# A hybrid decoder layer on one core: an early rope rotation on GpSimd, its casts behind the first query, and both heads' transposes ahead of the state products

## The chip, the cores and the metric

The kernel runs on one NeuronCore of a Trainium2 chip. The metric is device time in microseconds of one execution, from runs on the chip. The engines are TensorE (PE, matmuls and transposes; its weight loads are listed as PEld), VectorE (DVE), ScalarE (ACT), GpSimd (POOL) and SyncE (SP, which only issues DMAs here). Each engine works through its own queue in order; engines wait for one another through semaphores.

## The reference

One layer on 512 tokens of width 1024. Two branches read the same normalised input: HGRN2, a gated linear recurrence with 8 heads of 128, and multi-head latent attention (MLA) with 8 heads. Both are gated and merged; a projection, the residual and a last norm follow.

```python
h = rms_norm(x, norm_g[l]); proj = h @ w_in[l]
hq, hf, hi, hz, cq, ckv, kr, mz, glog = jnp.split(proj, pts, axis=-1)
y_a = hgrn2_branch(hq, hf, hi, hz, lower_bounds[l], hg_norm_g[l])
y_b = mla_branch(cq, ckv, kr, mz, ...)
merged = gates[:, :, 0] * (y_a @ w_proj_a[l]) + gates[:, :, 1] * (y_b @ w_proj_b[l])
x = x + merged @ w_out[l]
...
# HGRN2, in chunks of 32 tokens, per head
f = lb + (1 - lb) * sigmoid(hf); q = silu(hq); k = 1 - f; log_f = log(f)
b = cumsum(log_f)                                  # within a chunk
q_in, k_in, k_out = q * exp(b), k * exp(-b), k * exp(b_last - b)
o_intra = tril(q_in k_in^T) v
state = state * decay + k_out^T v;  o_inter = q_in state
...
# MLA: queries with a rope part of 64 columns per head
q_nope = q[..., :128];  q_pe = apply_rope(q[..., 128:], cos, sin)
s = (q_nope k_nope^T + q_pe k_pe^T) * scale; p = softmax(s); out = p v
```

`apply_rope` turns pairs of columns: x1 cos - x2 sin, x2 cos + x1 sin.

## The kernel before

Channels lie on the 128 partitions and the 512 tokens on the free axis. Large products are made from float32 split in two parts (`hi`, a cast on ScalarE at L118, and `lo`, a subtraction on VectorE at L119); `mm3` issues three matmuls (L91 to L93) for each pair of blocks. Weights come through `load_w`: a DMA into one of 3 raw buffers, then the two parts into one of 4 buffers each.

After the start, the HGRN2 heads are worked two at a time by `hg_pair` (pairs 0 to 3). A pair projects the forget gates (`pf`), runs `hg_forget` for each head, projects the values (in pairs 0 and 2) or the gate `z` (in 1 and 3), projects the queries and runs `hg_query` for each head, then `hg_states`, `hg_scores`, `hg_out` and `hg_gate`.

- `hg_forget`: tanh on ScalarE (L455), `f` on VectorE, `k` and `fr` on GpSimd (L458, L457), a scan and a reciprocal on VectorE (L460, L461), nine tiny products of chunk decays on GpSimd (`gh`, `ft`, L466 to L474), then `ki`, `ko` and `k128` on VectorE and `k64` on GpSimd (L478). `tf`, `f` and `k` have one buffer each.
- `hg_query`: tanh (L486), then `q`, `qi`, `q128` on VectorE and `q64` on GpSimd (L490).
- `hg_states`, one head: three transposes of `k128` on PE (L499), one ScalarE copy of the result to `kt` (L500, one buffer), three products with the values on PE (L504), and the running sums `st` on VectorE (L505, L508).
- `hg_scores`: three groups of small matmuls (L518, L524, L529) and four masked copies on VectorE (L533). `hg_out` (L542, L544) reads their result and `st`.

PSUM is used in banks of 128x512 float32: 3 for `mm_tile` (projections) and 5 for `ax_tile` (the rest), given out in turn.

The MLA queries' rope part is made for two heads at once. `mla_turn` projects it (`qr`) and makes a copy with swapped halves through DMAs from ScalarE's queue (`qs`). `mla_rotate` makes the rotation on GpSimd: two products with the table (L637, L638), their sum (L639), and two DMAs from GpSimd's queue that swap the partition halves into `qx`, which takes the buffer of `qs` (L642). `mla_rope` makes the parts that matmuls read: on ScalarE a cast of `qx` to `qh` (L650) and of the halves of `qr` to `qp` (L653), on VectorE two subtractions (L654). `mla_nope` makes the other query part and the keys of one head: 15 matmuls, and casts `qn`, `kn`.

For the first pair of MLA heads this is done inside the last HGRN2 pair: `mla_turn(0)` before it, the rotation as `after_forget` (behind both heads' `hg_forget`), and `mla_rope` and `mla_nope(0)` as `before_gate` (behind `hg_states`). `step` issues, from GpSimd's queue, DMAs that add blocks of later weights to one another in DRAM (L767).

The order on each queue is set when the program is built, by a list scheduler with its own cost estimates; only where the code says `manual_schedule` or `issue_after` is it bound by hand. `last_pool`, `last_act` and `last_dve` hold instructions behind which an `issue_after` places others.

Of the kernel before, what the change touches and what calls it, by code (L numbers as in the profile page):

```python
# [14 lines left out]
ALU = mybir.AluOpType  # L15
# [3 lines left out]
P = 128  # L19
D = 1024  # L20
S = 512
NT = S // P
KD = D // P
H = 8
# [14 lines left out]
def hybrid_layer(ctx: ExitStack, tc: tile.TileContext, a):  # L39
    nc = tc.nc  # L40
# [16 lines left out]
    def ax_tile():  # L57
        return ax.tile([P, 512], F32, tag="ax", name="ax_ps")
# [68 lines left out]
    def proj_ch(mat, c0, rhs, hook=None):  # L127

        ps = [mm_tile() for _ in range(2)]
        for kh, w in enumerate(load_cols(mat, c0)):  # L130
            for m in range(2):
                if hook and kh and m:
                    hook()
                for k in range(4):
                    kk = 4 * kh + k
                    mm3(ps[m][:], w, rhs, (slice(None), k, slice(m * P, m * P + P)),
                        (slice(None), kk), kk == 0, kk == KD - 1)
        return ps
# [17 lines left out]
    last_pool, last_dve, last_act = [None], [None], [None]  # L156
# [247 lines left out]
    kt = cw.tile([P, NT, NR], F32, "kt")  # L404
# [31 lines left out]
    for i in range(2):  # L436
        gh = hw.tile([P, NT, 12], F32, f"gh{i}")
# [5 lines left out]
    W = lambda tag, bufs=2, shape=(P, S): hw.tile(list(shape), F32, tag, bufs)  # L443
# [4 lines left out]
    def bc(gh, o, n):  # L448
        return gh[:, :, o : o + n].rearrange("p g (n o) -> p g n o", o=1).broadcast_to([P, NT, n, C])

    def hg_forget(h, pf):

        gh = gh_[h % 2]
        tf, f, k = W("tf", 1), W("f", 1), W("k", 1)
        nc.scalar.activation(tf[:], pf[:], AF.Tanh, scale=0.5)  # L455
        nc.vector.tensor_scalar(f[:], tf[:], c1[:, h : h + 1], c2[:, h : h + 1], op0=ALU.mult, op1=ALU.add)
        nc.gpsimd.tensor_scalar(fr[:, ::C], f[:, ::C], TINY, None, op0=ALU.max)  # L457
        nc.gpsimd.tensor_scalar(k[:], tf[:], c1n[:, h : h + 1], c1[:, h : h + 1], op0=ALU.mult, op1=ALU.add)  # L458
        pr, rp = W("pr"), W("tf", 1)
        nc.vector.tensor_tensor_scan(pr[:], f[:], fr[:], 0.0, op0=ALU.mult, op1=ALU.max)  # L460
        nc.vector.reciprocal(rp[:], pr[:])  # L461
        last = pr[:, C - 1 :: C]
        F = last.rearrange("p (g c) -> p g c", c=4)

        g = nc.gpsimd
        cp = lambda o, i: g.tensor_copy(gh[:, :, o], F[:, :, i])  # L466
        ml = lambda o, x, y: g.tensor_tensor(gh[:, :, o], x, y, op=ALU.mult)
        cp(2, 3), cp(5, 0), cp(8, 1), cp(11, 2)
        ml(1, F[:, :, 2], F[:, :, 3])
        ml(0, F[:, :, 1], gh[:, :, 1])  # L470
        ml(6, F[:, :, 0], F[:, :, 1])
        ml(7, gh[:, :, 6], F[:, :, 2])
        ft = W("ft", 2, (P, NT))
        g.tensor_tensor(ft[:], gh[:, :, 6], gh[:, :, 1], op=ALU.mult)  # L474
        ki, ko, k128, k64 = W("ki"), W("ko"), W("k128"), W("k64", 2, (P, S // 2))
        nc.vector.tensor_tensor(ki[:], k[:], rp[:], op=ALU.mult)
        nc.vector.tensor_tensor(c3(ko), c3(ki), last.rearrange("p (n o) -> p n o", o=1).broadcast_to([P, S // C, C]), op=ALU.mult)
        last_pool[0] = g.tensor_tensor(c2_(k64), c4(ko)[:, :, 0:2], bc(gh, 8, 2), op=ALU.mult)  # L478
        nc.vector.tensor_tensor(c4(k128), c4(ko), bc(gh, 0, 4), op=ALU.mult)
        return pr, ft, ki, ko, k64, k128  # L480

    def hg_query(h, pq, pr):

        gh = gh_[h % 2]
        q = W("f", 1)
        last_act[0] = nc.scalar.activation(q[:], pq[:], AF.Tanh, scale=0.5)  # L486
        nc.vector.scalar_tensor_tensor(q[:], q[:], 1.0, pq[:], op0=ALU.add, op1=ALU.mult)
        qi, q128, q64 = W("qi"), W("q128"), W("q64", 2, (P, S // 2))
        nc.vector.tensor_tensor(qi[:], q[:], pr[:], op=ALU.mult)
        last_pool[0] = nc.gpsimd.tensor_tensor(c2_(q64), c4(qi)[:, :, 2:4], bc(gh, 10, 2), op=ALU.mult)  # L490
        last_dve[0] = nc.vector.tensor_tensor(c4(q128), c4(qi), bc(gh, 4, 4), op=ALU.mult)
        return qi, q64, q128

    def hg_states(h, k128, ft, v_sb):

        kps, kt_ = ax_tile(), W("kt", 1)
        n3 = 3 * P
        for i in range(NT - 1):
            nc.tensor.transpose(kps[:, i * P : i * P + P], k128[:, i * P : i * P + P], ident[:])  # L499
        nc.scalar.copy(kt_[:, :n3], kps[:, :n3])  # L500
        sps, st_ = ax_tile(), W("st", 2, (P, n3))
        for i in range(NT - 1):
            sl = slice(i * P, i * P + P)
            nc.tensor.matmul(sps[:, sl], kt_[:, sl], v_sb[i][:, (h % 4) * P : (h % 4) * P + P], start=True, stop=True)  # L504
        nc.vector.tensor_copy(st_[:, 0:P], sps[:, 0:P])  # L505
        for i in range(1, NT - 1):
            sl, sp = slice(i * P, i * P + P), slice(i * P - P, i * P)
            nc.vector.scalar_tensor_tensor(st_[:, sl], st_[:, sp], ft[:, i : i + 1], sps[:, sl], op0=ALU.mult, op1=ALU.add)  # L508
        return st_
# [55 lines left out]

    v_sb = [None] * NT

    def hg_pair(pair, after_forget=None, before_gate=None, last=None):
        cc, hs = pair * 256, (2 * pair, 2 * pair + 1)
        pf = proj_ch(w_in, COL_F + cc, hT)  # L570
        kk = [hg_forget(h, pf[i]) for i, h in enumerate(hs)]
        if after_forget:
            after_forget()
        if pair:
            step()
        else:
            early_sums(kh[0])
        def gate():
            pz = proj_ch(w_in, COL_ZA + cc, hT)
            zz = [z_tile() for _ in hs]  # L580
            for i in range(2):
                silu2(zz[i][:], pz[i][:])
            return zz

        if pair % 2 == 0:
            for t in range(NT):
                v_sb[t] = hw.tile([P, 512], F32, f"v{t}")
            proj_tok(w_in, COL_I + cc, hT, lambda t, ps: nc.scalar.copy(v_sb[t][:], ps[:]))
        else:
            zz = gate()  # L590
        pq = proj_ch(w_in, COL_Q + cc, hT)
        qq = [hg_query(h, pq[i], kk[i][0]) for i, h in enumerate(hs)]
        step()
        sts = [hg_states(h, kk[i][5], kk[i][1], v_sb) for i, h in enumerate(hs)]
        if before_gate:
            before_gate()
        if pair % 2 == 0:
            zz = gate()
        def scores():
            return hg_scores([(h, kk[i][2:5] + qq[i][0:2]) for i, h in enumerate(hs)])  # L600

        def outs(aa):
            on = [hg_out(h, aa[i], sts[i], qq[i][2], v_sb) for i, h in enumerate(hs)]
            step()
            return on

        def gated(on):
            for i, h in enumerate(hs):
                hg_gate(h, on[i], zz[i])

        if last:
            return last(scores, outs, gated)
        gated(outs(scores()))
# [29 lines left out]
        last_pool[0] = turn  # L643
        return qr, qx

    def mla_rope(qr, qx):

        qp, qh = [ma_pool.tile([P, S], F32R, f"qp{i}") for i in range(2)], ma_pool.tile([P, S], F32R, "qh")
        with tc.issue_after(last_act[0].ins), tc.issue_after(last_dve[0].ins):
            nc.scalar.copy(qh[:], qx[:])  # L650
            for i in range(2):
                own, other = slice(64 * i, 64 * i + 64), slice(64 - 64 * i, 128 - 64 * i)
                nc.scalar.copy(qp[i][own], qr[own])  # L653
                nc.vector.tensor_tensor(qp[i][other], qx[other], qh[other].bitcast(F32), op=ALU.subtract)  # L654
        return qp

    def mla_values(h0):

# [153 lines left out]
    def step():  # L812
        if adds and last_pool[0]:
            x = adds.pop(0)
            if x:
                x[0].add(x[1])
# [8 lines left out]
    early = []  # L825

    def first_scores():
        early.append(mla_rope(*turned_q))
        early.append(mla_nope(0, ma_pool))

    def last_outputs(scores, outs, gated):
# [8 lines left out]
    turned_q = list(mla_turn(0))  # L840

    def rotate():
        turned_q[:] = mla_rotate(*turned_q)

    z = hg_pair(H // 2 - 1, rotate, first_scores, last_outputs)
    hw.close()

    def a_parts(src, to):
# [71 lines left out]
    qp, nope, pn = early  # L920
    late = None
    turned_q = mla_turn(1)
    for h in range(H):
        pools = (ma_pool, mw)
        if h in (2, 4):
            turned_q = mla_turn(h // 2 + 1)
        if h:
            pn = mla_scores(h, pools[h % 2], *nope, qp, h + 1 == H)
        if h % 2 and h + 1 < H:
            qp = mla_rope(*turned_q)  # L930
        if h:
            z = mla_gate(h)
# [14 lines left out]
        elif h:  # L947
            late = (h, hook(), v, z)
            if h in (2, 4):
                turned_q = mla_rotate(*turned_q)  # L950
            step()
        else:
# [4 lines left out]
            turned_q = mla_rotate(*turned_q)  # L957
# [4 lines left out]
    hs = Pool("h_sums", "right")  # L962
# [63 lines left out]
    for n, c in enumerate((0, 2, 1, 3)):  # L1026
        for i, ps in enumerate(proj_ch(a["w_proj_b"][0], c * 256, ybs)):
            j = 2 * c + i
            g = g1[j]
# [193 lines left out]
```

## Time and profile before

| | |
|---|---|
| median of 3 runs | 618.98 us (618.0 to 619.43) |
| the profiled execution | 618.9 us, of which the span from first to last instruction is 617.1 us |
| mean granted PE clock | 0.99 of full speed |
| PE busy | 602.9 us (98%), 3686 matmuls |
| VectorE, ScalarE, GpSimd busy | 435.5, 286.0, 152.1 us |
| pair 3, from its first forget tanh to its last score group | 226.74 to 267.0 us of the span |

All durations in the prediction come from that one profiled execution. Rows of a timeline give start, length, engine, line, operation, output and inputs, shape and count; in brackets stands how long the engine was idle before and what ended that. Matmuls overlap by pipelining, so their lengths exceed the step from one to the next.

### The profile page before, as it was taken

Reading aid. Unit: us, or ns where it says so; the run is one execution under the profiler, and the core shown is the slowest. Engines: PE = TensorE matmul, PEld = TensorE weight load, DVE = VectorE, ACT = ScalarE, POOL = GpSimd, SP = SyncE. Lnnn points to the kernel's source line nnn. Section 1 sums busy time; section 2 is a strip of 40 time slices with the busy share of each in tenths; the row PEclk is TensorE's granted clock in tenths of the full one; section 3 lists DMA queues with packets and bytes.
Section 4 is the critical chain, followed back from the end, with each engine's and each line's share of the span. In section 5 each row is a group of like instructions: output and inputs, shape, how many; then the busy total and the mean of one; then the engine's idle time right before and its main releaser. Section 6 shows DMA issues by size and latency. Waiting matters only on the chain.

```text
span 617.1 us, 9789 instructions
## 1 busy us (share of the span) xinstructions
PE 602.9 (98%) x3686; PEld 529.2 (86%) x3686; DVE 435.5 (71%) x679; ACT 286.0 (46%) x531; POOL 152.1 (25%) x253
## 2 busy tenths in 40 slices
PE   8999999999999999799999999999999999999994
PEld 5998888888888888688888888899999999888884
DVE  7727989499864549927767776647766678667885
ACT  5554244323143242426555454547657754424352
POOL 4106322444350142806245430400000000000011
PEclk9999999999999999989999999999999999999998
DMA  7549479987969964682379576766655655695103
GB/s 265 167 134 345 144 239 367 293 210 170 284 129 311 213 144 98 146 162 60 64 160 165 129 177 136 181 242 215 206 175 178 203 179 167 206 354 180 45 32 137
DMA packets 74543, 114.37 MB, mean 185 GB/s; under 512 B 7512, under 2 KB 41726, under 8 KB 74496
## 3 DMA queue, kind: packets, MB, share of 16 engines
q1 hardware_dynamic: 65100, 89.69, 45.1%
q0 software_dynamic: 8336, 22.55, 19.9%
q10 hardware_dynamic: 1060, 1.51, 0.7%
q8 instruction: 29, 0.48, 0.3%
q14 instruction: 18, 0.15, 0.1%
HBM read 105.34 MB, written 39.85 MB: 235 GB/s over the span
## 4 chain that ended last, share of the span: by engine, by line
PE 85%; DVE 7%; ACT 2%; POOL 2%; issue 2%; DMA 1%; POOLq 0%; ACTq 0%; DVEq 0%
PE mm_ps L91 17%; PE mm_ps L92 17%; PE mm_ps L93 17%; PE ax_ps L862 16%; PE mm_ps L862 3%; PE ax_ps L700 2%; DVE w_lo L119 1%; PE mm_ps L271 1%; PE ax_ps L724 1%; PE ax_ps L542 1%; DVE tf L461 1%; DVE ya L1094 1%; PE ax_ps L92 1%; PE ax_ps L93 1%; PE ax_ps L91 1%
## 5 line engine op out<-in xcount | busy, mean ns | idle before, releaser
L119 DVE TENSOR_TENSOR w_lo<-w_raw,w_hi 128x1024 fp32r<-128x1024 f32 (+3 forms) x116 | 137.7, 1201 | 77.8 <-ACT w_hi L118 72.2
L118 ACT CAST w_hi<-w_raw 128x1024 fp32r<-128x1024 f32 (+3 forms) x116 | 114.7, 1005 | 141.7 <-PE mm_ps L92 67.3
L91 PE MATMUL mm_ps<-hT,w_hi 128*128 128x512 f32 x320 | 125.5, 394 | 0.0
L92 PE MATMUL mm_ps<-hT,w_hi 128*128 128x512 f32 x320 | 125.1, 391 | 0.0
L93 PE MATMUL mm_ps<-hT,w_lo 128*128 128x512 f32 x320 | 124.8, 392 | 0.0
L93 PEld LDWEIGHTS mm_ps<-hT,w_lo 128*128 128x128 f32 x320 | 60.1, 188 | 12.4
L91 PEld LDWEIGHTS mm_ps<-hT,w_hi 128*128 128x128 f32 x320 | 60.1, 188 | 11.9
L92 PEld LDWEIGHTS mm_ps<-hT,w_hi 128*128 128x128 f32 x320 | 60.1, 188 | 11.8
L862 PE MATMUL ax_ps<-s,w_hi 128*128 128x256 f32 x384 | 54.1, 283 | 0.0
L862 PEld LDWEIGHTS ax_ps<-s,w_hi 128*128 128x128 f32 x384 | 49.7, 192 | 0.1
L1111 POOL TENSOR_SCALAR ssum<-ssum 128x1 f32<-128x1 f32 x3 | 0.9, 308 | 188.5 <-ACT sq L1098 188.5
L93 PE MATMUL mm_ps<-w_hi,hT 128*128 128x512 f32 (+1 forms) x96 | 36.6, 383 | 0.0
L92 PE MATMUL mm_ps<-w_lo,hT 128*128 128x512 f32 (+1 forms) x96 | 36.5, 382 | 0.0
L91 PE MATMUL mm_ps<-w_hi,hT 128*128 128x512 f32 (+1 forms) x96 | 36.4, 386 | 0.0
L706 ACT ACTIVATE p<-ax_ps,sm 128x128 f32<-128x128 f32 (+3 forms) x32 | 16.8, 527 | 34.4 <-DVE sm L705 31.0
L708 POOL TENSOR_SCALAR p<-p,sm 128x128 f32<-128x128 f32 (+3 forms) x28 | 15.5, 556 | 66.1 <-DVE sm L705 41.3
L862 PE MATMUL ax_ps<-s,w_lo 128*128 128x256 f32 x192 | 31.3, 284 | 0.2 <-DVE w_lo L119 0.2
L862 PEld LDWEIGHTS ax_ps<-s,w_lo 128*128 128x128 f32 x192 | 26.6, 192 | 0.4 <-DVE w_lo L119 0.4
L461 DVE RECIPROCAL tf<-pr 128x512 f32<-128x512 f32 x8 | 26.8, 3348 | 0.1
L91 PE MATMUL mm_ps<-cT,w_hi 128*128 128x512 f32 x52 | 20.6, 397 | 0.0
L91 PEld LDWEIGHTS mm_ps<-w_hi,hT 128*128 128x128 f32 x96 | 18.0, 188 | 3.0
L93 PEld LDWEIGHTS mm_ps<-w_hi,hT 128*128 128x128 f32 x96 | 18.0, 188 | 3.0
(299 smaller groups left out, 1221.1 us busy)
## 6 DMA issues: line engine op xcount, KB each, us to landing
w_raw<-w_in SPq DMA_DIRECT2D x54, 512.0 KB, 6.6
g_t<-w_in SPq DMA_DIRECT2D x16, 512.0 KB, 8.7
w_raw<-g_t SPq DMA_DIRECT2D x16, 512.0 KB, 4.5
g_t<-w_in POOLq DMA_DIRECT2D x8, 512.0 KB, 10.1
pa_t<-w_proj_a SPq DMA_DIRECT2D x8, 512.0 KB, 12.9
g_t<-g_t POOLq DMA_DIRECT2D x8, 512.0 KB, 11.0
out_t<-w_out SPq DMA_DIRECT2D x8, 512.0 KB, 8.3
s<-h POOLq DMA_DIRECT2D x8, 512.0 KB, 11.8
```

The costliest lines, as they stand in the source:

```text
L91: nc.tensor.matmul(ps, lh[lsl], rh[rsl], start=start, stop=False)
L92: nc.tensor.matmul(ps, lh[lsl], rl[rsl], start=False, stop=False)
L93: nc.tensor.matmul(ps, ll[lsl], rh[rsl], start=False, stop=stop)
L118: last_hi[0] = nc.scalar.copy(hi[:, :o], raw[:, :o])
L119: last_lo[0] = nc.vector.tensor_tensor(lo[:, :o], raw[:, :o], hi[:, :o].bitcast(F32), op=ALU.subtract)
L271: nc.tensor.matmul(ps, hT[l][:, 4 * kh + k, t * P : t * P + P], c_hl[kh][r][:, k * 256 : k * 256 + 256], start=kh == 0 and kind == 0 and k ...
L461: nc.vector.reciprocal(rp[:], pr[:])
L542: nc.tensor.matmul(ops[:, sl], asb[:, sl], v_sb[i][:, (h % 4) * P : (h % 4) * P + P], start=True, stop=i == 0)
L700: nc.tensor.matmul(sps[:, :n], qh[:, bl], kpe[x][:, :n], start=False, stop=x == 1)
L706: last_act[0] = nc.scalar.activation(p[:, :n], sps[:, :n], AF.Exp, scale=SCALE, bias=sm[:, 1:2], accum_out=sm[:, 2:3])
L708: scaled_p = (nc.vector if final else nc.gpsimd).tensor_scalar(p[:, :n], p[:, :n], sm[:, 3:4], 0.5, op0=ALU.mult, op1=ALU.mult)
L862: nc.tensor.matmul(ps[:, o], w[k // 2][i][:, k % 2, cols], ap[j][:, k], start=not banks and c == 0 and n == 0, stop=n == 11, skip_group_ch ...
```

## The change

`hg_forget` and `hg_query` take a function, `meanwhile`, that issues something in their midst; `hg_pair` hands it to the first head only. The last pair gives `rotate` to `hg_forget`, which calls it behind the first head's `ft`, and `cast` to `hg_query`, which calls it behind the first query's tanh. `mla_rope` is cut in two: `mla_rope_hi` holds the casts on ScalarE and `mla_rope_lo` the subtractions on VectorE, which stay in `first_scores`. In every pair `hg_states` loses its transposes and copy to a new `hg_turned`, which runs for both heads first; `kt` gets two buffers of 384 columns.

```diff
-    def hg_forget(h, pf):
+    def hg_forget(h, pf, meanwhile=None):
...
-        g.tensor_tensor(ft[:], gh[:, :, 6], gh[:, :, 1], op=ALU.mult)
+        last_pool[0] = g.tensor_tensor(ft[:], gh[:, :, 6], gh[:, :, 1], op=ALU.mult)
+        if meanwhile:
+            meanwhile()
...
-    def hg_query(h, pq, pr):
+    def hg_query(h, pq, pr, meanwhile=None):
...
         last_act[0] = nc.scalar.activation(q[:], pq[:], AF.Tanh, scale=0.5)
+        if meanwhile:
+            meanwhile()
...
-    def hg_states(h, k128, ft, v_sb):
-
-        kps, kt_ = ax_tile(), W("kt", 1)
-        n3 = 3 * P
+    n3 = (NT - 1) * P
+
+    def hg_turned(k128):
+
+        kps, kt_ = ax_tile(), W("kt", 2, (P, n3))
         for i in range(NT - 1):
             nc.tensor.transpose(kps[:, i * P : i * P + P], k128[:, i * P : i * P + P], ident[:])
-        nc.scalar.copy(kt_[:, :n3], kps[:, :n3])
+        last_act[0] = nc.scalar.copy(kt_[:], kps[:, :n3])
+        return kt_
+
+    def hg_states(h, kt_, ft, v_sb):
+
         sps, st_ = ax_tile(), W("st", 2, (P, n3))
...
-    def hg_pair(pair, after_forget=None, before_gate=None, last=None):
+    def hg_pair(pair, in_forget=None, in_query=None, before_gate=None, last=None):
...
-        kk = [hg_forget(h, pf[i]) for i, h in enumerate(hs)]
-        if after_forget:
-            after_forget()
+        kk = [hg_forget(h, pf[i], None if i else in_forget) for i, h in enumerate(hs)]
...
-        qq = [hg_query(h, pq[i], kk[i][0]) for i, h in enumerate(hs)]
+        qq = [hg_query(h, pq[i], kk[i][0], None if i else in_query) for i, h in enumerate(hs)]
         step()
-        sts = [hg_states(h, kk[i][5], kk[i][1], v_sb) for i, h in enumerate(hs)]
+        kts = [hg_turned(k[5]) for k in kk]
+        sts = [hg_states(h, kts[i], kk[i][1], v_sb) for i, h in enumerate(hs)]
...
-    def mla_rope(qr, qx):
+    def mla_rope_hi(qr, qx):
...
-        with tc.issue_after(last_act[0].ins), tc.issue_after(last_dve[0].ins):
+        with tc.issue_after(last_act[0].ins):
             nc.scalar.copy(qh[:], qx[:])
             for i in range(2):
-                own, other = slice(64 * i, 64 * i + 64), slice(64 - 64 * i, 128 - 64 * i)
+                own = slice(64 * i, 64 * i + 64)
                 nc.scalar.copy(qp[i][own], qr[own])
+        return qp, qh, qx
+
+    def mla_rope_lo(qp, qh, qx):
+
+        with tc.issue_after(last_dve[0].ins):
+            for i in range(2):
+                other = slice(64 - 64 * i, 128 - 64 * i)
                 nc.vector.tensor_tensor(qp[i][other], qx[other], qh[other].bitcast(F32), op=ALU.subtract)
         return qp
...
     def first_scores():
-        early.append(mla_rope(*turned_q))
+        early.append(mla_rope_lo(*turned_q))
...
+    def cast():
+        turned_q[:] = mla_rope_hi(*turned_q)
+
-    z = hg_pair(H // 2 - 1, rotate, first_scores, last_outputs)
+    z = hg_pair(H // 2 - 1, rotate, cast, first_scores, last_outputs)
```

GpSimd's queue in pair 3 before: from the second head's last decay product to its `q64`. `k64`, `q64` are the 128x256 products; the weight additions are the L767 DMAs; `gh1` belongs to the second head, and the numbers tell tiles apart.

```order
L474 TENSOR_TENSOR ft_2372<-gh1_641 128x4
L478 TENSOR_TENSOR k64_2377<-ko_2375,gh1_641 128x256
L637 TENSOR_TENSOR qr_2253<-qr_2253,qtab_630 128x512
L638 TENSOR_TENSOR qs_2254<-qs_2254,qtab_630 128x512
L639 TENSOR_TENSOR qr_2253<-qr_2253,qs_2254 128x512
L490 TENSOR_TENSOR q64_2529<-qi_2527,gh0_637 128x256
L642 DMA qs_2385<-qr_2253 64x512 x2
L767 DMA g1_t4_652<-g1_t2_650 128x1024 x2
L490 TENSOR_TENSOR q64_2538<-qi_2536,gh1_641 128x256
```

The same queue after, from the first head's last decay product (`gh0`) on:

```order
L474 TENSOR_TENSOR ft_2343<-gh0_637 128x4
L645 TENSOR_TENSOR qr_2253<-qr_2253,qtab_630 128x512
L646 TENSOR_TENSOR qs_2254<-qs_2254,qtab_630 128x512
L647 TENSOR_TENSOR qr_2253<-qr_2253,qs_2254 128x512
L650 DMA qs_2348<-qr_2253 64x512 x2
L480 TENSOR_TENSOR k64_2354<-ko_2352,gh0_637 128x256
L458 TENSOR_SCALAR k_2361<-tf_2359,c1n_424,c1_423 128x512
L457 TENSOR_SCALAR fr_635<-f_2360 128x16
```

The rotation and its DMAs moved from behind the second head's `k64` to ahead of the first head's.

ScalarE's queue in pair 3 before, from the first query's tanh (`f`) to the second `kt` copy (`w_hi` are weight casts, `qn`, `kn` the casts of `mla_nope(0)`):

```order
L486 ACTIVATE f_2524<-mm_ps_2460 128x512
L118 CAST w_hi_2841<-w_raw_2840 128x640
L486 ACTIVATE f_2533<-mm_ps_2461 128x512
L653 CAST qp0_2572<-qr_2253 64x512
L653 CAST qp1_2573<-qr_2253 64x512
L500 COPY kt_2545<-ax_ps_2544 128x384
L160 CAST qn0_2597<-mm_ps_2587 128x512
L118 CAST w_hi_2873<-w_raw_2872 128x1024
L160 CAST kn0_2608<-mm_ps_2601 128x512
L650 CAST qh_2574<-qs_2385 128x512
L500 COPY kt_2559<-ax_ps_2558 128x384
```

And after:

```order
L488 ACTIVATE f_2524<-mm_ps_2460 128x512
L658 CAST qh_2528<-qs_2348 128x512
L661 CAST qp0_2526<-qr_2253 64x512
L661 CAST qp1_2527<-qr_2253 64x512
L118 CAST w_hi_2841<-w_raw_2840 128x640
L488 ACTIVATE f_2539<-mm_ps_2461 128x512
L505 COPY kt_2551<-ax_ps_2550 128x384
L505 COPY kt_2557<-ax_ps_2556 128x384
L160 CAST qn0_2597<-mm_ps_2587 128x512
L118 CAST w_hi_2873<-w_raw_2872 128x1024
L160 CAST kn0_2608<-mm_ps_2601 128x512
```

The three casts of the rotation moved up behind the first tanh, and the two `kt` copies stand side by side ahead of `qn`.

PE's queue in pair 3 before, from the end of `mla_nope(0)`'s 15 matmuls to the first score group:

```order
L93 MATMUL mm_ps_2601<-cT0_91,w_lo_2582 128x512
L504 MATMUL ax_ps_2550<-v0_1815,kt_2545 128x128
L504 MATMUL ax_ps_2550<-v1_1816,kt_2545 128x128
L504 MATMUL ax_ps_2550<-v2_1817,kt_2545 128x128
L499 MATMUL ax_ps_2558<-ident_105,k128_2376 128x128 x3
L504 MATMUL ax_ps_2564<-v0_1815,kt_2559 128x128
L504 MATMUL ax_ps_2564<-v1_1816,kt_2559 128x128
L504 MATMUL ax_ps_2564<-v2_1817,kt_2559 128x128
L518 MATMUL ax_ps_2614<-qi_2527,ki_2345 64x64 x8
```

And after, ahead of those 15 matmuls, where before only the first head's transposes stood (`k128_2353` is the first head's, `k128_2382` the second's):

```order
L93 MATMUL mm_ps_2461<-hT0_125,w_lo_2471 128x512
L504 MATMUL ax_ps_2550<-ident_105,k128_2353 128x128 x3
L504 MATMUL ax_ps_2556<-ident_105,k128_2382 128x128 x3
L91 MATMUL mm_ps_2587<-cT0_91,w_hi_2581 128x512
L92 MATMUL mm_ps_2587<-cT1_92,w_hi_2581 128x512
```

The second head's transposes moved ahead of the 15 matmuls; behind these the six products now follow without a transpose between them. In pairs 0 to 2 the second head's transposes moved ahead of the first head's products in the same way, and in pair 1 the products and scores of both heads moved 24 projection matmuls forward.

More of the change, by code (lines that the diff above doesn't have):

```diff
@@ L644, in mla_rotate, with mla_rope @@
         return qr, qx
-    def mla_rope(qr, qx):
+    def mla_rope_hi(qr, qx):
         qp, qh = [ma_pool.tile([P, S], F32R, f"qp{i}") for i in range(2)], ma_pool.tile([P, S], F32R, "qh")
-        with tc.issue_after(last_act[0].ins), tc.issue_after(last_dve[0].ins):
+        with tc.issue_after(last_act[0].ins):
             nc.scalar.copy(qh[:], qx[:])
             for i in range(2):
-                own, other = slice(64 * i, 64 * i + 64), slice(64 - 64 * i, 128 - 64 * i)
+                own = slice(64 * i, 64 * i + 64)
                 nc.scalar.copy(qp[i][own], qr[own])
+        return qp, qh, qx
[3 more added lines that the diff above has]
+                other = slice(64 - 64 * i, 128 - 64 * i)
                 nc.vector.tensor_tensor(qp[i][other], qx[other], qh[other].bitcast(F32), op=ALU.subtract)
         return qp
+    def mla_rope(qr, qx):
+        return mla_rope_lo(*mla_rope_hi(qr, qx))
     def mla_values(h0):
```

## The prediction

> **What bounds the kernel now.** The page first: its line of busy times.
>
> ```profile
> PE 602.9 (98%) x3686; PEld 529.2 (86%) x3686; DVE 435.5 (71%) x679; ACT 286.0 (46%) x531; POOL 152.1 (25%) x253
> ```
>
> TensorE (PE) is busy for 98% of the span, so a change can only pay where PE stands still or is clocked down. The list of waits, for PE alone, is the second view: apart from the start-up it has two entries, and only the first has weight (microseconds in sum, times, longest).
>
> ```profile
> PE ax_ps L504 <- ACT kt L500: 3.8, 2, 3.4
> ...
> PE ax_ps L862 <- DVE w_lo L119: 0.2, 1, 0.2
> ```
>
> PE's state products (L504) waited for ScalarE's copy of the transposed keys (L500) twice in the whole run, 3.8 us in sum. PE's own timeline places both in the last pair of heads. One row per group; the bracket is PE's idle time before it and what ended it:
>
> ```profile
> 251.73 0.39 PE L93 MATMUL mm_ps<-hT,w_lo 128*128 128x512 f32 x1
> 251.96 0.49 PE L499 MATMUL ax_ps<-ident,k 128*128 128x128 f32 x3
> ...
> 256.30 0.94 PE L504 MATMUL ax_ps<-v,kt 128*128 128x128 f32 x6 [0.39 <-ACT kt L500]
> 257.07 0.49 PE L499 MATMUL ax_ps<-ident,k 128*128 128x128 f32 x3
> 260.99 0.80 PE L504 MATMUL ax_ps<-v,kt 128*128 128x128 f32 x2 [3.43 <-ACT kt L500]
> ```
>
> So 0.39 us before the first head's products and 3.43 us before the second's. (The first two rows also give PE's step: a 512-wide matmul starts 0.23 us after the one ahead of it.) Third, a table of stretches, with the granted clock in the column PEclk:
>
> ```profile
> core 0: us, PE busy (x) PEld busy (x) DVE busy (x) ACT busy (x) POOL busy (x), PEclk, DMA share, GB/s
> ...
> 257.50:261.00 3.50, 0.07 (x2) 0.01 (x1) 3.36 (x6) 1.79 (x4) 3.50 (x5) 0.80 0.98 201
> 261.00:267.00 6.00, 6.00 (x87) 5.53 (x87) 2.60 (x7) 0.00 (x0) 1.36 (x2) 0.55 1.08 195
> 267.00:278.00 11.00, 11.00 (x64) 9.64 (x64) 3.18 (x5) 3.84 (x15) 0.74 (x2) 1.00 0.69 145
> ```
>
> The stall has a second price: in the 6 us behind it PE is fully busy at a clock of 0.55, and back at 1.00 from 267. What that costs shows in the chain of waits, where the same four groups of pair 2 and pair 3 can be laid side by side (start, length, group):
>
> ```profile
> 209.66 0.67 PE ax_ps L504 x6
> 210.33 1.08 PE ax_ps L518 x32
> 211.41 0.63 PE ax_ps L524 x32
> 212.04 1.07 PE ax_ps L529 x16
> ...
> 256.22 3.65 DMA qs<-qr
> ...
> 260.99 1.65 PE ax_ps L504 x6
> 262.64 1.91 PE ax_ps L518 x32
> 264.55 1.00 PE ax_ps L524 x32
> 265.55 1.49 PE ax_ps L529 x16
> ```
>
> 3.45 us of work (0.67 + 1.08 + 0.63 + 1.07) took 6.05 us: 2.60 us lost. The stall's cause stands in ScalarE's timeline; its queue runs in order:
>
> ```profile
> 249.44 0.60 ACT L486 ACTIVATE f<-mm_ps 128x512 f32<-128x512 f32 x1 [1.52 <-PE mm_ps L93]
> ...
> 252.61 0.59 ACT L486 ACTIVATE f<-mm_ps 128x512 f32<-128x512 f32 x1
> 254.50 1.25 ACT L653 CAST qp<-qr 64x512 fp32r<-64x512 f32 x2 [1.29 <-POOL qr L639]
> 255.77 0.48 ACT L500 COPY kt<-ax_ps 128x384 f32<-128x384 f32 x1
> ...
> 259.94 0.62 ACT L650 CAST qh<-qs 128x512 fp32r<-128x512 f32 x1 [1.65 <-DMA qs<-qr]
> ```
>
> The first kt copy sits behind the casts of qp, which wait for GpSimd's rotation; the second sits behind the cast of qh, which waits for the rotation's DMA. The rotation is late because GpSimd does it last.
>
> **The change, part by part.**
>
> *Rotation between the first head's gates and its k64 (GpSimd).*
>
> ```profile
> 231.35 0.20 POOL L474 TENSOR_TENSOR ft<-gh 128x4 f32<-128x4 f32 x1
> 237.19 1.07 POOL L478 TENSOR_TENSOR k<-ko,gh 128x256 f32<-128x256 f32 x1 [5.64 <-DVE ko L477]
> ...
> 249.45 1.61 POOL L637 TENSOR_TENSOR qr<-qr,qtab 128x512 f32<-128x512 f32 x1
> ...
> 255.57 1.20 POOL L642 DMA_DIRECT2D qs<-qr  x2
> ```
>
> GpSimd stood idle for 5.64 us from 231.55. Into that go three products and two DMA issues. Those three took 4.97 us here (249.45 to 254.42) and the issues 1.20, 6.2 us in all, so at these lengths GpSimd is free at 237.7, 0.5 us later than its k64 started. The other instances of the same product are shorter:
>
> ```profile
> L637 POOL TENSOR_TENSOR qr<-qr,qtab x4: 1287/1292/1609, 249.4 to 349.4; 128x512 f32<-128x512 f32 x4
> ```
>
> At the median of 1.29 us GpSimd is done at about 236.6 and delays nothing by itself. The DMA lands 3.65 us after its issue (chain row), near 241; at the worst of it, a start at 237.7 and twice that time, 245. It is needed at 250.04, when the first query's tanh ends.
>
> Queued behind the rotation on GpSimd: k64 of head 0, then k, fr and the gates of head 1; VectorE's scan of head 1 waits for fr. On VectorE the first head's chain goes on meanwhile:
>
> ```profile
> 230.67 3.34 DVE L461 RECIPROCAL tf<-pr 128x512 f32<-128x512 f32 x1
> ...
> 234.50 1.22 DVE L119 TENSOR_TENSOR w_lo<-w_raw,w_hi 128x1024 fp32r<-128x1024 f32 x1
> ...
> 236.96 0.82 DVE L119 TENSOR_TENSOR w_lo<-w_raw,w_hi 128x640 fp32r<-128x640 f32 x1
> ...
> 248.31 0.69 DVE L479 TENSOR_TENSOR k<-ko,gh 128x512 f32<-128x512 f32 x1
> ...
> 253.23 1.92 DVE L119 TENSOR_TENSOR w_lo<-w_raw,w_hi 128x640 fp32r<-128x640 f32 x1
> ```
>
> The same 640-wide subtraction takes 0.82 us with GpSimd quiet and 1.92 beside the rotation: 1.10 us of contention. That cost moves along: I take one such delay, 1.0 us, for the w_lo at 234.50 or the ki behind it, and the reciprocal as unhurt. So head 1's k128, done at 249.00, comes at 250.0. No row shows the reciprocal beside a long GpSimd product. Its bounds: no delay, or stretched like that subtraction (1.92/0.82), 3.34 x 1.34 = 4.5 us more; I take the lower end, since the products elsewhere on GpSimd are as short as 1.29 us and since the reciprocal, unlike that subtraction, reads one tensor. The Trainium skill, "SBUF — State Buffer", section "Who interferes with whom", says that a VectorE instruction contends with a GpSimd one that reads SBUF if it has two SBUF inputs or runs in a two-port mode. By that rule the reciprocal goes free and w_lo, ki and ko pay, which is the lower end; the two rows of 0.82 and 1.92 agree with it, and the reciprocal is not tested here.
>
> *Both heads' transposes first.* PE reaches them at 251.96 and needs head 1's k128 at about 252.3: 2.3 us spare. The 15 nope matmuls follow (3.45 us), then the products at 255.91 + 0.33 = 256.24, 0.33 being the second head's transposes done early. That adds no work.
>
> *Casts behind the first query's tanh (ScalarE).* qh, qp, qp now wait for nothing: 250.04 + 0.62 + 1.25 = 251.9, the w_hi cast behind them started at 251.97 already. Second tanh to 253.2, the two kt copies of 0.48 to 254.2, against 256.24: 2.0 us spare. kt now has two buffers, so the second copy waits for no product. Queued behind the casts are that tanh and both copies; the landing near 241 covers them, and gone by 2 us past 250.04 it would put PE back into waiting.
>
> *qp's two subtractions on VectorE* now precede the first head's state sums and stand behind both heads' qi and q128. PE reads the sums only with the outputs, after the whole score block and 23 matmuls (5.3 us); hidden by those.
>
> *Pairs 0 to 2.* PE waited for kt only in pair 3, so nothing is to be had there; only order moves. Closest is pair 1, where the scheduler now puts both heads' products and scores 24 matmuls earlier, at about 144.50 + 0.33 + 0.7 + 0.33 + 21 x 0.23 = 150.7:
>
> ```profile
> 144.50 0.49 PE L499 MATMUL ax_ps<-ident,k 128*128 128x128 f32 x3
> ...
> 147.17 0.48 ACT L500 COPY kt<-ax_ps 128x384 f32<-128x384 f32 x1
> ...
> 150.28 0.62 POOL L490 TENSOR_TENSOR q<-qi,gh 128x256 f32<-128x256 f32 x1 [2.49 <-DVE qi L489]
> ...
> 108.93 2.40 DVE L533 COPY_PREDICATED asb<-mask_le,ax_ps 64x512 f32<-64x512 uint8 x4
> ```
>
> Both kt copies end by 148.2 (2.5 spare); GpSimd's q64 by 150.9, used at 150.7 + 1.34 + 1.08 + 0.63 = 153.7 (2.8 spare); scores end near 154.8, the four masked copies take 2.4 (pair 0's row) to 157.2, and PE, after 22 matmuls (5.1 us), needs them at 159.9 (2.7 spare). Cost nothing.
>
> **Sum.** 0.39 + 3.43 of waiting and 2.60 of slow clock: 6.42 us. PE's list of waits shows nothing later but the 0.2 us, and what follows runs on PE's heels, so the gain should reach the end. The profiled execution took 618.9 us (span 617.1): 618.9 - 6.4 = 612.5. It lies within 0.1 us of the runs' median (618.98), so that needs no shift.
>
> **Rivals.**
>
> 1. *The wait moves to head 1's transposes.* If the reciprocal pays the upper bound, k128 comes at 250.0 + 4.5 = 254.5, 2.2 us after PE needs it. For it: GpSimd now works beside the longest VectorE instruction of the pair. Against: the median of 1.29 us. Price: 2.2 us, hence 614.7; if the clock drops again, 2.6 more, 617.3. The Trainium skill, "TensorE: Matmul & The Clock Gate", section "What's actually happening", has the clock halved after a free-running idle window of about 3.4 us. By that rule a wait of 2.2 us keeps the clock and the time is 614.7; the stall of 3.43 us with 0.55 behind it agrees.
>
> 2. *It does not do what it says.* The DMA lands late, behind the 512 KB additions that GpSimd issues in the same queue, so kt still waits behind qh. It decides at a landing past 252; near 256 the whole gain is gone: 618.9. Against: 9 us between 241 and 250.
>
> 3. *Slower: pair 1's hand-over.* There the masked copies stand in VectorE's queue behind a w_lo whose raw weights and cast must be in time. Late by the 2.7 us spare plus 3.8 us, PE idles 3.8 and loses 2.6 to the clock: the gain is spent. At 5 us of idle it is 612.5 + 5 + 2.6 = 620.1. Against: none of its inputs was a wait of PE before.
>
> **Chances.** Full gain 0.75 (own range 611.0 to 613.8); rival 1, or a similar small wait elsewhere, 0.12 (613.8 to 617.3); rival 2, 0.06; rival 3, 0.07. A change of 0.2%, 1.2 us, is about what can be told from none. Faster 0.86, same 0.07, slower 0.07. The range, 611.0 to 617.0, leaves out rivals 2 and 3 and the top of rival 1.
>
> **What would show it.** Right: no PE wait for kt, PEclk 1.00 throughout 250 to 270, the rotation on GpSimd at about 231.6, the qh cast right behind the first tanh with no DMA wait, the score groups (L518 before) at 1.08 us, and everything behind them about 6.4 us earlier. Wrong: a PE wait at the pair-3 transposes for VectorE's k128, a reciprocal well above 3.35 us, or a new PE gap between 144 and 172.

## Result: 612.44 us against 618.95, and the profile after

The changed kernel takes 612.44 us in the median of 4 runs (612.32 to 613.25), the kernel before 618.95 beside it (618.0 to 619.43). The ratio is 0.9901, 95% interval [0.9889, 0.9913]: 6.5 us less. The profiled execution took 612.32 us, its span 610.5 us.

The page's busy times and clock row of the changed kernel:

```profile
PE 600.0 (98%) x3686; PEld 526.6 (86%) x3686; DVE 434.5 (71%) x679; ACT 285.4 (47%) x531; POOL 151.8 (25%) x253
...
PEclk9999999999999999999999999999999999999998
```

PE was busy for 602.9 us before and is for 600.0 now, with the same 3686 instructions: most of the 2.9 us (2.33, worked out below) is work that ran at a slow clock. The rest of the gain is waiting. PE's list of waits has lost its entry for `kt`; what remains is the start-up (L236, L271, L260) and the old 0.2 us:

```profile
PE ax_ps L236 <- DVE zero L282: 1.2, 1, 1.2
PE mm_ps L271 <- DVE w_lo L243: 0.5, 1, 0.5
PE ax_ps L260 <- DVE xn L252: 0.4, 1, 0.4
PE ax_ps L883 <- DVE w_lo L119: 0.2, 1, 0.2
```

PE's timeline in the last pair of heads (start, length, group) has no bracket of idle time left, and the score groups have their quick lengths:

```profile
251.97 0.82 PE L504 MATMUL ax_ps<-ident,k 128*128 128x128 f32 x6
...
256.08 1.50 PE L513 MATMUL ax_ps<-v,kt 128*128 128x128 f32 x12
257.51 1.15 PE L527 MATMUL ax_ps<-qi,ki 128*64 128x64 f32 x32
258.59 0.70 PE L533 MATMUL ax_ps<-qi,ko 128*32 128x32 f32 x32
259.22 1.15 PE L538 MATMUL ax_ps<-q,k 128*64 128x64 f32 x16
260.30 0.50 PE L91 MATMUL mm_ps<-hT,w_hi 128*128 128x512 f32 x1
```

The table of stretches says the same of the clock (PEclk, third from the end), where it stood at 0.80 and 0.55 before:

```profile
257.50:261.00 3.50, 3.50 (x84) 3.22 (x84) 3.50 (x8) 0.13 (x1) 0.75 (x1) 1.00 1.09 263
261.00:267.00 6.00, 6.00 (x35) 5.17 (x34) 4.21 (x8) 1.53 (x2) 0.00 (x0) 1.00 1.07 184
```

ScalarE's timeline shows why. No cast waits for the rotation or its DMA any more, and both `kt` copies are done at 253.96, 2.1 us ahead of the products:

```profile
249.45 0.60 ACT L488 ACTIVATE f<-mm_ps 128x512 f32<-128x512 f32 x1 [1.52 <-PE mm_ps L93]
249.94 0.61 ACT L658 CAST qh<-qs 128x512 fp32r<-128x512 f32 x1
250.45 1.25 ACT L661 CAST qp<-qr 64x512 fp32r<-64x512 f32 x2
251.99 0.73 ACT L118 CAST w_hi<-w_raw 128x640 fp32r<-128x640 f32 x1 [0.28 <-ACT qp L661]
252.62 0.59 ACT L488 ACTIVATE f<-mm_ps 128x512 f32<-128x512 f32 x1
253.11 0.85 ACT L505 COPY kt<-ax_ps 128x384 f32<-128x384 f32 x2
```

### The profile page after: what moved, and what is told of

It reads as the page before. It is cut to its first block, busy times and chain, and to the rows that moved or that the text cites. A ratio compares the mean times of both kernels' runs of the same rounds, so it can differ in the third digit from the quotient of the medians.

```text
span 610.5 us, 9790 instructions
## 1 busy us (share of the span) xinstructions
PE 600.0 (98%) x3686; PEld 526.6 (86%) x3686; DVE 434.5 (71%) x679; ACT 285.4 (47%) x531; POOL 151.8 (25%) x253
## 4 chain that ended last, share of the span: by engine, by line
PE 89%; DVE 6%; ACT 2%; issue 1%; DMA 0%; POOL 0%; POOLq 0%; ACTq 0%; DVEq 0%
PE mm_ps L91 19%; PE mm_ps L92 19%; PE mm_ps L93 19%; PE ax_ps L883 16%; PE mm_ps L883 3%; PE ax_ps L718 2%; PE mm_ps L271 1%; PE ax_ps L742 1%; PE ax_ps L551 1%; DVE w_lo L119 1%; DVE ya L1115 1%; PE ax_ps L93 1%; PE ax_ps L92 1%; PE ax_ps L91 1%; PE ax_ps L553 1%
```

## The experiments

The change has three parts: the rotation in the first head's gates (R), the casts behind the first query (C), the transposes of both heads ahead (T). The medians of the kernel before beside these runs were 618.95, 618.89 (T, R, R and C, one line) and 618.35 (the others).

| kernel | us, median | ratio to before, interval | PE's wait for `kt` in the profile |
|---|---|---|---|
| changed: R, C and T | 612.44 | 0.9901 [0.9889, 0.9913] | none |
| R and T | 612.41 | 0.9906 [0.9892, 0.9921] | none |
| T | 613.62 | 0.9916 [0.9902, 0.993] | none (0.41 behind `kn`) |
| R | 613.74 | 0.9919 [0.9906, 0.9931] | 0.93 |
| C and T | 613.77 | 0.9928 [0.9917, 0.994] | 1.16 |
| R and C | 613.81 | 0.9919 [0.9904, 0.9933] | 0.82 |
| one line (below) | 614.13 | 0.9925 [0.9912, 0.9937] | 0.82 |

**The transposes' part alone.** The copy now stands in `hg_turned`, `kt` has two buffers.

```diff
-        nc.scalar.copy(kt_[:, :n3], kps[:, :n3])
+        last_act[0] = nc.scalar.copy(kt_[:], kps[:, :n3])
...
-        sts = [hg_states(h, kk[i][5], kk[i][1], v_sb) for i, h in enumerate(hs)]
+        kts = [hg_turned(k[5]) for k in kk]
+        sts = [hg_states(h, kts[i], kk[i][1], v_sb) for i, h in enumerate(hs)]
```

> Only the transposes' part: both heads' key transposes and kt copies stand ahead of the state products; the rotation and its casts stay late as before. Theory (PE waited because the kt copies stood behind the casts in ScalarE's queue, and only for that): the copies now stand ahead of the casts and end near 254.2, the products start near 256.2 without a wait, PEclk stays at 1.00, about 612.4. The late rotation by itself costs nothing, since its results are first read by the attention scores. Rival (the late rotation itself holds something up, so that it must move early): a wait of PE is left near 260, 616 to 618.9.

Measured: 613.62 us (613.04 to 614.47); most of the gain, 1.2 us short of what the theory expected. The wait for `kt` is gone, as it said, but the late rotation does hold something else up. ScalarE's timeline (start, length, instruction):

```profile
254.53 1.26 ACT L659 CAST qp<-qr 64x512 fp32r<-64x512 f32 x2 [0.55 <-POOL qr L645]
...
260.18 0.62 ACT L656 CAST qh<-qs 128x512 fp32r<-128x512 f32 x1 [3.78 <-DMA qs<-qr]
260.71 1.05 ACT L118 CAST w_hi<-w_raw 128x1024 fp32r<-128x1024 f32 x1
261.66 0.58 ACT L160 CAST kn<-mm_ps 128x512 fp32r<-128x512 f32 x1
```

And PE's, at the matmul that had to wait for VectorE's subtraction of `kn`, which follows that cast:

```profile
264.43 0.50 PE L91 MATMUL mm_ps<-cT,w_hi 128*128 128x512 f32 x1 [0.41 <-DVE kn L161]
```

The `qh` cast stands 3.78 us waiting for the rotation's DMA, with a `w_hi` and the `kn` cast queued behind it, and PE waits 0.41 us behind `kn`. The waiting matmul doesn't read `kn` (its inputs are `cT` and `w_hi`); what it has in common with the subtraction is `mm_ps`, one of only three PSUM banks. That is the rival in small: "the late rotation by itself costs nothing" was wrong. The profiled execution, 613.04 us, was the quickest of the five. What the others lost beyond it no profile shows; a DMA that lands later would lengthen just this wait.

**The rotation's part alone.** Against the kernel before, `rotate` is called inside the first head's `hg_forget`; the casts stay in `first_scores`.

```diff
-    z = hg_pair(H // 2 - 1, rotate, first_scores, last_outputs)
+    z = hg_pair(H // 2 - 1, rotate, None, first_scores, last_outputs)
```

> Only the rotation's part: inside the first head's forget gates on GpSimd; the casts stay where the first scores begin, the transposes stay apart. Theory: the casts wait for nothing, so the first kt copy ends near 255.6 and the first wait (0.39 us) goes; the second copy stands in ScalarE's queue behind the qn cast, a w_hi cast and the kn cast, and ends near 258.8, while the transposes end near 257.3: a wait of about 1.4 us for kt, too short to drop the clock, about 613.8 to 614.2. Rival (the whole gain is the rotation's): 612.4. Rival (any wait of over 1 us drops the clock for 6 us): about 616.5.

Measured: 613.74 us (613.42 to 614.14). ScalarE's timeline:

```profile
255.54 0.48 ACT L504 COPY kt<-ax_ps 128x384 f32<-128x384 f32 x1
255.92 0.59 ACT L160 CAST qn<-mm_ps 128x512 fp32r<-128x512 f32 x1
256.54 1.05 ACT L118 CAST w_hi<-w_raw 128x1024 fp32r<-128x1024 f32 x1
257.49 0.58 ACT L160 CAST kn<-mm_ps 128x512 fp32r<-128x512 f32 x1
257.96 0.48 ACT L504 COPY kt<-ax_ps 128x384 f32<-128x384 f32 x1
```

PE's timeline beside it:

```profile
257.08 0.49 PE L503 MATMUL ax_ps<-ident,k 128*128 128x128 f32 x3
258.50 0.94 PE L508 MATMUL ax_ps<-v,kt 128*128 128x128 f32 x6 [0.93 <-ACT kt L504]
259.36 1.15 PE L522 MATMUL ax_ps<-qi,ki 128*64 128x64 f32 x32
```

The first wait is gone, the second is 0.93 us; it was expected at about 1.4. Only a part of it is ScalarE's queue: the transposes end at 257.57, and the copy starts at 257.96, behind three casts. The copy itself then takes 0.48 us, and PE waits for that too, since the products stand right behind their transposes; R can't take that part away, T can. The groups behind it have their quick lengths, so a wait of 0.93 us dropped no clock here.

**Rotation and casts, transposes apart.** Against the changed kernel, with `hg_states` as it was before:

```diff
-        kts = [hg_turned(k[5]) for k in kk]
-        sts = [hg_states(h, kts[i], kk[i][1], v_sb) for i, h in enumerate(hs)]
+        sts = [hg_states(h, kk[i][5], kk[i][1], v_sb) for i, h in enumerate(hs)]
```

> The changed kernel without its transposes' part: rotation early, casts behind the first query's tanh, but each head's transposes right ahead of its own products. Theory: like the rotation alone, since the second kt copy still stands behind the qn, w_hi and kn casts: one wait of 1.2 to 1.4 us for kt, clock 1.00, 613.6 to 614.2. Rival (casts ahead of the second tanh are what counts): 612.4.

Measured: 613.81 us (613.3 to 614.17), one wait of 0.82 us for `kt` (1.2 to 1.4 were expected), clock 1.00 throughout 252 to 278. Like the rotation alone: the casts' place adds nothing.

**One line.** Against the kernel before, the `kt` copy is taken as the last ScalarE instruction, behind which the casts are issued:

```diff
-        nc.scalar.copy(kt_[:, :n3], kps[:, :n3])
+        last_act[0] = nc.scalar.copy(kt_[:, :n3], kps[:, :n3])
```

> One line against the kernel before: the kt copy counts as the last ScalarE instruction, so that the casts of qp and qh are issued behind both kt copies; rotation late, transposes apart. Theory: the first copy ends near 253.7 (no wait), the second behind the qn, w_hi and kn casts near 258.7: one wait of 1.2 to 1.4 us, clock 1.00, 613.6 to 614.2, so that most of the gain is the order of two kinds of copy in ScalarE's queue. Rival (the rotation must be early): 617 to 618.9.

Measured: 614.13 us (613.86 to 614.45): 4.8 us of the 6.5 without moving the rotation or the transposes. PE's only wait in the pair, again shorter than the expected 1.2 to 1.4 us:

```profile
258.64 0.94 PE L504 MATMUL ax_ps<-v,kt 128*128 128x128 f32 x6 [0.82 <-ACT kt L500]
```

So the stall was an order of ScalarE's queue: urgent copies behind casts that waited for something late. Either making the casts not wait (R) or getting the copies out from behind them (T, which contains this line, or the line by itself) removes most of it. The parts don't add up: 5.2 us for R alone, 5.3 for T alone, 6.5 for the whole change.

**Rotation and transposes, casts left late.** Against the changed kernel; the casts stand in `first_scores` again.

```diff
-    z = hg_pair(H // 2 - 1, rotate, cast, first_scores, last_outputs)
+    z = hg_pair(H // 2 - 1, rotate, None, first_scores, last_outputs)
```

> The changed kernel with the casts left where the first scores begin: rotation early, both heads' transposes ahead. Theory: the kt copies are ahead of the casts and the rotation's DMA has long landed, so that neither the wait for kt nor the 0.41 us wait for kn, seen with the transposes' part alone (where a w_hi cast and the kn cast stood behind a qh cast that waited for the DMA until 260.2), is left: no wait of PE after the start-up but the 0.2 us, about 612.4. The casts' place is then worth nothing beside the other two parts. Rival (the casts must stand behind the first query's tanh): 613 to 614.

Measured: 612.41 us (612.22 to 612.94), no wait in the pair. The casts' part is worth nothing beside the other two; by itself it was not run.

**Casts and transposes, rotation left late.** Against the changed kernel:

```diff
-        kk = [hg_forget(h, pf[i], None if i else in_forget) for i, h in enumerate(hs)]
+        kk = [hg_forget(h, pf[i]) for i, h in enumerate(hs)]
+        if in_forget:
+            in_forget()
```

> The changed kernel with the rotation left late (behind both heads' forget gates): casts of qp behind the first query's tanh, both heads' transposes ahead. Theory: the qp casts now wait for the rotation in front of the second tanh and both kt copies: casts end near 255.8, w_hi, tanh near 257.0, copies near 257.5 and 258.0, against products at 256.1: a wait of 1.3 to 1.9 us for kt, no drop of the clock, 613.5 to 614.4; early casts without the early rotation lose what the transposes' part gains. Rival (the order of casts is harmless): 612.4 to 613.0.

Measured: 613.77 us (613.64 to 614.6). ScalarE's timeline:

```profile
254.77 1.25 ACT L663 CAST qp<-qr 64x512 fp32r<-64x512 f32 x2 [4.44 <-POOL qr L649]
256.05 0.73 ACT L118 CAST w_hi<-w_raw 128x640 fp32r<-128x640 f32 x1
256.68 0.59 ACT L488 ACTIVATE f<-mm_ps 128x512 f32<-128x512 f32 x1
257.17 0.85 ACT L505 COPY kt<-ax_ps 128x384 f32<-128x384 f32 x2
```

PE's first transposes in the pair, the row that waits for these copies, and the matmul behind the scores:

```profile
252.27 0.81 PE L504 MATMUL ax_ps<-ident,k 128*128 128x128 f32 x6
...
257.69 1.60 PE L513 MATMUL ax_ps<-v,kt 128*128 128x128 f32 x12 [1.16 <-ACT kt L505]
...
262.01 0.50 PE L91 MATMUL mm_ps<-hT,w_hi 128*128 128x512 f32 x1
```

The early casts carry their 4.44 us of waiting in front of the tanh and the copies: PE waits 1.16 us again, a little under the expected 1.3 to 1.9. The early rotation is what makes the casts' new place harmless.

**The clock's share: work put into the stall.** The kernel before, with matmuls whose result is overwritten, behind the second head's transposes:

```diff
+        if h == H - 1:
+            with tc.issue_after(turned.ins):
+                for _ in range(13):
+                    nc.tensor.matmul(sps[:], cT[0][:, 0, 0:P], cT[0][:, 1], start=True, stop=True)
```

> The kernel before with 13 idle-filling 128x512 matmuls (3.0 us, results overwritten) behind the second head's transposes of the last pair: TensorE waits as long for kt as before, but has work for most of the 3.43 us. Theory (the slow clock behind the stall is a price of its own, 2.6 us, and comes of TensorE standing still): PEclk stays at 1.00 in 261 to 267, the products start near 261 as before, and the time is 618.9 - 2.6 = 616.3. Rival (the slow matmuls behind the stall are slow for another reason, such as memory traffic at that time): 618.9.

Measured: 616.31 us (616.21 to 617.13), ratio 0.9969 [0.9957, 0.9981]: 13 more matmuls on the busiest engine made the kernel quicker. The clock stayed at 1.00, as the theory has it, but that the time hit 616.3 is in part luck: half of the first score group moved up into the wait (0.6 us), and the DMA let the `qh` cast go only at 260.95, 1.0 us later than before, so that the products started at 262.00 and not near 261. The profiled execution, 617.13 us, was the slowest of the five.

With 4 instead of 13:

> The same with 4 such matmuls (0.9 us): TensorE still stands still for some 2.5 us of the 3.43. Theory with a threshold between 0.93 us (a wait that left the clock at 1.00 with the rotation's part alone) and 3.43: if 2.5 us are under it, the clock stays at 1.00 and the time is 616.3 as with 13; if not, 618.9. Rival (the loss grows with the length of the idle time, 2.6 us for 3.43): 1.9 us are lost, 618.2.

Measured: 616.25 us, spread from 615.36 to 619.04 over 12 runs. As a test of a 2.5 us wait it failed: 38 score matmuls had moved up into it and PE stood still for 0.81 us only in the profiled execution (615.45 us, clock 1.00 in that stretch). Four of the 12 runs, 617.84 to 619.04 us, had a mean clock of 0.993 where the others had 0.995 to 0.997; none of these four was profiled. So the scores were then held behind the products:

```diff
+            with tc.issue_after(last_prod[0].ins):
+                return hg_scores(heads)
```

> The same with 7 filling matmuls (1.6 us), the score matmuls held behind the products: TensorE stands still for about 1.8 us. If about 2 us of standing still halve the clock, and no less: 616.3 with the clock at 1.00. If any wait of over 1 us does: 618.9. With a free-running window: mostly 616.3.

Measured: 616.52 us (616.25 to 616.73), ratio 0.997 [0.9958, 0.9982]. This is the clean one; PE's timeline:

```profile
257.53 1.87 PE L507 MATMUL ax_ps<-cT 128*128 128x512 f32 x7
260.92 0.94 PE L510 MATMUL ax_ps<-v,kt 128*128 128x128 f32 x6 [1.52 <-ACT kt L502]
261.78 1.15 PE L524 MATMUL ax_ps<-qi,ki 128*64 128x64 f32 x32
...
264.57 0.50 PE L91 MATMUL mm_ps<-hT,w_hi 128*128 128x512 f32 x1
```

The products start at 260.92, as before (260.99), but the hT matmul behind the scores follows 3.65 us later instead of 5.98: 2.33 us less for the same matmuls, behind a shorter standstill. The slow clock is a price of its own, and it comes of the standing still. Memory traffic is not its cause: between 261 and 267 the DMA engines are as busy in the changed kernel, at a clock of 1.00, as before (1.07 and 1.08 in the last column but one).

Against the median of the kernel before beside these runs, 618.24, the gain is 1.7 us, less than that 2.33. Only one execution of the kernel before was profiled, and in the 44 beside the experiments the time and the mean clock go together: 0.989 to 0.992 in the nine above 619 us, 0.992 to 0.995 in the eleven below 618. So the clock's price differs from one execution to the next, and the profiled one (618.9 us, 0.99) is among the dearer: 12 of the 44 took as long or longer.

With 4 filling matmuls and the scores held:

> As with 4 filling matmuls, but the last pair's score matmuls are held behind the second head's state products (in the run before, 38 of them had moved up into the wait and shortened it to 0.81 us), so that TensorE really stands still for about 2.5 us. The trace of the kernel before has the clock at 0.50 from 2.04 us after TensorE's last work (257.56 to 259.60) until 266.42, that is for 6.82 us. If standing still for about 2 us is what halves the clock: PEclk falls within the wait, 618.9. If it takes the 3.4 us of the original stall: clock 1.00, 616.3. If it depends on where the wait falls against a window that runs freely: some executions near 616.3 and some near 618.9.

Measured: 617.91 us in the median, ratio 0.9988 [0.9979, 0.9997], and in two groups: three of 12 runs at 616.22 to 616.56, nine at 617.80 to 618.69. The profiled one (617.81) is of the second group:

```profile
260.82 1.65 PE L510 MATMUL ax_ps<-v,kt 128*128 128x128 f32 x6 [2.38 <-ACT kt L502]
262.40 1.84 PE L524 MATMUL ax_ps<-qi,ki 128*64 128x64 f32 x32
...
265.87 0.50 PE L91 MATMUL mm_ps<-hT,w_hi 128*128 128x512 f32 x1
```

From the products to the hT matmul it took 5.05 us, against 3.65 with 7 filling matmuls and 5.98 before: standing still for 2.38 us cost 1.40 us of slow clock where 3.43 us cost 2.33, and in a quarter of the runs, by their times, it seems, nothing. Of the three answers in the expectation, the freely running window fits best.

## Why the prediction was right, point by point

The forecast was 612.5 us, the measurement 612.44. The mechanism was right; that the two lie within 0.1 us is in part luck, since the sum of 6.42 us was 0.25 short of the 6.67 that the profiles show, and the changed kernel's median lies 0.12 above its profiled execution (612.32). The time after held because the forecast took the price of the stall from the same execution, 618.9 us, in which it had read it. The gain depends on the runs of the kernel before: 6.5 us here, but 5.9 for R and T (612.41) against 618.35 us in 17 runs.

- **The waits, 0.39 + 3.43 us.** Right, both gone.
- **The slow clock, 2.60 us.** Right in kind: the stretch is at 1.00, and the filled stall shows the term by itself. Its size is 2.33: from 260.99 to 266.97 PE needed 5.98 us, and for the same matmuls behind a wait at full clock 3.65 (258.50 to 262.15 in R, 260.92 to 264.57 with 7 filling matmuls). The rows of pair 2, from which 3.45 was taken, have no wait ahead of them.
- **"That adds no work".** Right, and joining the groups saved none either: six transposes took 0.58 us (251.97 to 252.55) and twelve products 1.43 (256.08 to 257.51), against 0.25 for three and 0.67 for six in R's run.
- **A term that the sum left out, 0.53 us.** A stop of PE costs more than the idle time in its bracket. The last matmul ahead of it counts as work for its whole length, 0.39 us, where the next would have followed after 0.23, and the matmuls behind it start slowly: the twelve products took 1.54 us in C and T, where they waited, and take 1.43 now. From the first transposes to the hT matmul behind the scores PE now needs 8.33 us (251.97 to 260.30). With one stop it needed 9.74 in C and T (1.16 in the bracket), 9.53 in R (0.93), 9.42 in R and C and in the one line (0.82): 0.25 to 0.27 us on top of the bracket each time, whether the groups were joined or not. The kernel before had two stops, and its 15.01 us (251.96 to 266.97) are 8.33 + 3.82 + 2.33 of slow clock + 0.53. So the hT matmul starts 6.67 us earlier; the span is 6.6 us shorter, the medians differ by 6.5. The forecast of 256.24 for the products shows the same slip: it goes by the end of the last matmul, 255.91, and not by its start and one step; they started at 256.08.
- **GpSimd.** It starts the rotation at 231.57 and ends its issues at 236.96 (forecast 236.6). The three products and the issues:

```profile
231.57 1.28 POOL L645 TENSOR_TENSOR qr<-qr,qtab 128x512 f32<-128x512 f32 x1
...
234.17 1.29 POOL L647 TENSOR_TENSOR qr<-qr,qs 128x512 f32<-128x512 f32 x1
235.76 1.20 POOL L650 DMA_DIRECT2D qs<-qr  x2 [0.30 <-POOL qr L647]
238.02 1.07 POOL L480 TENSOR_TENSOR k<-ko,gh 128x256 f32<-128x256 f32 x1 [1.06 <-DVE ko L479]
```

 The `k64` behind it still waits for VectorE, 1.06 us: GpSimd delays nothing by itself.
- **The reciprocal**, the widest unknown, took the lower bound; `w_lo` paid:

```profile
230.73 3.35 DVE L461 RECIPROCAL tf<-pr 128x512 f32<-128x512 f32 x1
...
234.55 1.98 DVE L119 TENSOR_TENSOR w_lo<-w_raw,w_hi 128x1024 fp32r<-128x1024 f32 x1
```

 3.35 us beside the rotation and 3.34 without; `w_lo` 1.98 against 1.22, so the contention was 0.76 us where 1.0 was taken. The Trainium skill, "SBUF — State Buffer", section "Who interferes with whom", whose rule let the reciprocal with its one input go free and made a subtraction of two inputs pay, agrees with both rows. One reading of the prediction doesn't hold: beside its row of 0.82 us (236.96) GpSimd was not quiet, since the `k64` of 237.19 ran beside most of it; the rows that set an idle GpSimd against a busy one are those of 1.22 and 1.98. Head 1's `k128` ends at 249.82 (forecast 250.0), 2.2 us before PE's transposes begin.
- **Pair 1.** Products at 150.60 (forecast 150.7), scores end at 154.81 (154.8), masked copies at 156.86 (157.2), with the outputs that read them at 159.93 and no gap on PE.
- **Rival 1** did not occur, and one clause of it would have been unsafe: that a wait of 2.2 us keeps the clock. The filled stall kept it at 1.52 us and lost it at 2.38 in the profiled run.
- **What the prediction did not ask** is which parts were needed. It argued the three together. The runs show that two ways out existed and the change takes both: T is needed because R alone leaves 0.93 us, R because T alone leaves 0.41, and C is not needed beside them.

## What to carry to other kernels

When the bounding engine waits for a quick copy, look at what stands ahead of the copy in its engine's queue, and what that waits for; here one ordering line brought 4.8 of 6.5 us, and an instruction that must wait should stand behind all that is ready. Price a stall of the bounding engine with the clock behind it: 3.43 us of standing still cost another 2.33 us of slow clock in the profiled execution, 1.52 us cost none in its own. And count a stop dearer than its bracket: each cost some 0.25 us more here.

## What the runs showed of the clock

The clock doesn't follow the stall in proportion. The kernel before, in stretches of its stall (PEclk third from the end):

```profile
258.00:259.60 1.60, 0.00 (x0) 0.00 (x0) 1.60 (x3) 0.29 (x1) 1.60 (x4) 1.00 1.01 166
259.60:266.40 6.80, 5.41 (x79) 5.00 (x80) 3.46 (x8) 1.00 (x2) 2.76 (x3) 0.50 1.04 191
266.40:267.00 0.60, 0.60 (x11) 0.53 (x10) 0.39 (x1) 0.00 (x0) 0.00 (x0) 0.98 1.02 169
```

PE's last work ended at 257.56, so the clock fell 2.0 us into the stall, and stayed at half for 6.8 us, though PE was at work again after 1.4 of them. In the kernel with 4 filling matmuls and the scores held, it fell near 260.5 and was back near 263.95, 3.4 us:

```profile
260.50:260.60 0.10, 0.00 (x0) 0.00 (x0) 0.10 (x1) 0.10 (x1) 0.10 (x2) 0.69 1.24 246
...
263.90:264.00 0.10, 0.10 (x8) 0.10 (x6) 0.00 (x0) 0.00 (x0) 0.00 (x0) 0.74 1.08 172
```

6.8 is twice 3.4. The Trainium skill, "TensorE: Matmul & The Clock Gate", section "What's actually happening", has the clock set by how busy PE was, over windows of about 3.4 us that run freely. One and two windows of half clock, and runs of one kernel in two groups, agree with that; that it takes a whole window of standing still, as the prediction had read it, doesn't, if a window ended where the clock fell: the 3.4 us ahead of 259.60 hold 1.26 us of PE's work. Where the windows lie in other executions no run here shows.
